# The end of a log-sum-exp kernel: clearing the semaphores on ScalarE during the last store, and waiting for that store behind the exit barriers

## The chip, the cores and the metric

The kernel runs on one core of a Trainium2 chip. The metric is the device time of one execution in microseconds; each time quoted is the median of several executions. The profile calls the engines PE (TensorE), DVE (VectorE), ACT (ScalarE), POOL (GpSimd) and SP (SyncE). All times inside a trace count from the start of the span, which is the time from the first to the last instruction of the program.

## The reference

```
def setup_inputs():
    batch, seq, dim = 32, 512, 1024
    return {"x": np.random.randn(batch, seq, dim).astype(np.float32), "axis": -1}

def reference(x, axis):
    x_max = np.max(x, axis=axis, keepdims=True)
    return (x_max.squeeze(axis) + np.log(np.sum(np.exp(x - x_max), axis=axis))).astype(np.float32)
```

There are 16,384 rows of 1,024 values: 67 MB come in and 64 KB go out.

## The kernel before

The rows are spread over 128 partitions, 128 rows on each. SyncE loads them in 17 chunks into a ring. ScalarE takes the exponentials; some rows are summed by ScalarE in the same instruction, the others by VectorE. Two logarithms, one early and one at the end, turn the sums into results, and ScalarE issues the one store:

```
    landed = [tc.alloc_semaphore(f"landed{i}") for i in range(len(CHUNKS))]
    act_done = tc.alloc_semaphore("act_done")
    dve_done = tc.alloc_semaphore("dve_done")
    stored = tc.alloc_semaphore("stored")
    # ... loads, exponentials, sums ...
    take_logs(logged, NB, dves, acts)
    nc.scalar.wait_ge(act_done, acts)
    nc.scalar.dma_start(out=out_v, in_=res).then_inc(stored, 16)
    nc.gpsimd.wait_ge(stored, 16)
    # ... the instruction lists are put in order; the function ends ...
```

What the program does behind its last line matters here. The semaphores came from the tile context, so the context's exit adds, after the wait: an all-engine barrier, a range clear on GpSimd that sets these 20 semaphores to zero (in the trace before, one update of each of the semaphores 99 to 118, from 161.765 to 161.856 us), and a second all-engine barrier. In such a barrier four engines each add one to a "gather" semaphore; GpSimd waits for all four, then adds four to a "release" semaphore, on which the others wait. For the first barrier the trace before shows four updates of semaphore 96 (the last, ScalarE's, at 160.212 us), GpSimd's decrement of it at 161.498 us, its addition to semaphore 97 at 161.576 us, and four decrements of that from 161.610 to 161.668 us.

The softmax here doesn't subtract the row's maximum and nothing guards it: scores larger than these inputs give would overflow.

## Time and profile before

| | before |
|---|---|
| time, median of 6 runs | 164.21 us (163.94 to 164.43) |
| span of the profiled run | 162.2 us |
| last logarithm ends | 159.61 us |
| store issued, and its last semaphore increment | 159.64, 161.215 us |
| last instruction ends | 162.18 us |

These are lines of the page of the kernel before: the span, the busy time of each engine with its share and number of instructions, and the chain of work that ended last.

```profile
span 162.2 us, 213 instructions
...
DVE 72.9 (45%) x11; ACT 124.1 (76%) x136; POOL 0.2 (0%) x4
...
ACT 52%; DMA 38%; DVE 7%; issue 1%
```

The loads bound the first part and ScalarE the second. The chain of waits of the kernel before shows this in order of time; its columns are start, duration (us), and what the chain ran through.

```profile
47.15 36.52 DMA ring<-in_x_dram
83.67 0.02 issue
83.69 10.55 ACT ring L128 x21
...
156.21 2.71 ACT ring L128 x5
158.91 0.22 issue
159.14 0.20 ACT ring L128
159.34 0.02 issue
159.36 0.25 ACT res L93
```

From about 84 us on, the chain stays on ScalarE, and it ends with the last logarithm (L93) at 159.61 us. But the span is 162.2 us. The last 2.6 us hold no counted work, so the chain and the shares of busy time don't describe them. The last two lines of the timeline of the kernel before (start, duration, engine, line, operation) show what is left:

```profile
159.36 0.25 ACT L93 ACTIVATE res<-sums 128x61 f32<-128x61 f32 x1
159.64 0.37 ACTq L140 DMA_DIRECT2D out_dram<-res  x1
```

The rest is barrier work, all of it put down to the line that launches the program (L189). These are six of the twelve lines of that line's view for the kernel before (left out are drains and semaphore instructions of other engines). In a barrier, the DRAIN of four engines carries their addition to the gather semaphore, and GpSimd has one ahead of its wait. The columns are engine, instruction, count, shortest/median/longest duration in ns, first and last start.

```profile
L189 POOLq EVENT_SEMAPHORE  x4: 17/17/17, 161.5 to 162.1; - x4
L189 POOLq DRAIN  x3: 34/41/83, 161.4 to 161.9; - x3
L189 ACTq DRAIN  x2: 8/80/152, 160.1 to 161.7; - x2
L189 PEldq EVENT_SEMAPHORE  x2: 51/51/51, 161.6 to 162.1; - x2
L189 POOLq COMPARE_BRANCH  x1: 33/33/33, 161.2 to 161.2; - x1
L189 POOLq EVENT_SEMAPHORE_RANGE_CLEAR  x1: 139/139/139, 161.7 to 161.7; - x1
```

GpSimd's branch at 161.2 carries the wait for the store. ScalarE was at the first barrier at 160.1 already (its first DRAIN), but everything of GpSimd's comes after 161.2. Taken one by one from the trace's instruction and semaphore records:

```
159.64  ScalarE  store issued (0.37 us)
160.21  ScalarE  gather mark of the first barrier
161.04 - 161.215 the store's 16 semaphore increments
161.24  GpSimd   wait for the store passes (branch), then a drain
161.58           first barrier released
161.74  GpSimd   range clear (0.14 us), then a drain
162.10           second barrier released
162.18  TensorE  last instruction ends: end of the span
```

From here on, the landing of the store is its last semaphore increment, at 161.215 here. So 0.96 us of serial work stand behind the landing, up to the end of the span. After the span the records show more: nine increments of semaphore 2 from 162.41 to 162.94, updates of many other semaphores from 162.83 on, then nine more increments of semaphore 2 from 163.73 to 164.083. No instruction of the program touches semaphore 2, so this text puts these increments down to the runtime; that is an inference. They are called its marks, the time from one to the next is a hop, the first nine are called the first closing barrier, and the stretch from the landing to the last mark is the tail. The reported time of this run is 163.96 us, 0.12 us less than the last mark.

### The profile page before, as it was taken

The page shows a single profiled execution, that of the slowest core. Times are in us where ns is not written, and L with a number is a line of the kernel's source. Part 1 is how long each engine was busy: PE and PEld are TensorE (multiplying, and loading weights), DVE is VectorE, ACT ScalarE, POOL GpSimd, SP SyncE. Part 2 cuts the span into 40 slices and gives each one's busy share as a digit, 9 for nine tenths or more (in the row PEclk, how much of TensorE's full clock was granted, in tenths as well). Part 3 has the DMA queues.
Part 4 walks back from the last instruction along what each step waited for, and adds up shares of the span by engine and source line. Part 5 has one row for each costly group of instructions (what it writes and reads, how often), then busy time and mean ns, then how long its engine had stood idle before and what let it go on. Part 6 is the DMA issues. An engine that isn't in the chain of part 4 may idle for free.

```text
span 162.2 us, 213 instructions
## 1 busy us (share of the span) xinstructions
DVE 72.9 (45%) x11; ACT 124.1 (76%) x136; POOL 0.2 (0%) x4
## 2 busy tenths in 40 slices
DVE  0030000039960799000999900000006999799591
ACT  3180006997099971999339999999999999999993
POOL 0000000000000000000000000000000000000000
DMA  6999899969969959969988999999999999999970
GB/s 263 497 485 470 349 394 517 485 291 517 485 291 517 517 259 517 517 275 501 517 368 370 424 424 432 461 497 388 436 427 399 431 400 439 420 424 414 415 318 16
DMA packets 2593, 67.18 MB, mean 414 GB/s; under 512 B 288, under 2 KB 416, under 8 KB 800
## 3 DMA queue, kind: packets, MB, share of 16 engines
q1 hardware_dynamic: 2448, 67.11, 96.4%
q10 hardware_dynamic: 144, 0.07, 0.1%
q14 instruction: 1, 0.01, 0.0%
HBM read 67.11 MB, written 0.07 MB: 414 GB/s over the span
## 4 chain that ended last, share of the span: by engine, by line
ACT 52%; DMA 38%; DVE 7%; issue 1%
DMA ring<-in_x_dram 38%; ACT ring L128 30%; ACT ring L116 22%; DVE sums L121 7%; ACT res L93 0%
## 5 line engine op out<-in xcount | busy, mean ns | idle before, releaser
L121 DVE TENSOR_REDUCE sums<-ring 128x5 f32<-128x5120 f32 (+8 forms) x11 | 72.9, 6648 | 86.0 <-ACT ring L116 85.9
L116 ACT ACTIVATE ring<-ring 128x5120 f32<-128x5120 f32 (+8 forms) x11 | 59.3, 5394 | 29.4 <-DMA ring<-in_x_dram 29.4
L128 ACT ACTIVATE ring<-ring 128x1024 f32<-128x1024 f32 x61 | 63.4, 1041 | 5.3 <-DMA ring<-in_x_dram 5.3
L128 ACT ACTIVATION_READ_ACCUMULATOR ring<-ring 128x1 f32 x61 | 11.4, 187 | 0.0
L103 ACT ACT_TABLE_LOAD x1 | 1.3, 1283 | 0.8 <-PEq L175 0.8
L93 ACT ACTIVATE res<-sums 128x67 f32<-128x67 f32 (+1 forms) x2 | 0.5, 256 | 0.1
L175 POOL MEMSET const-bfloat16-1.0<- 128x1 bf16 x1 | 0.1, 101 | 0.0
L175 POOL MEMSET const-uint8-127<- 128x1 uint8 x1 | 0.1, 101 | 0.0
L175 POOL MEMSET const-float32-0.0<- 128x1 f32 x1 | 0.1, 98 | 0.2 <-issue 0.2
L175 POOL MEMSET const-float32-1.0<- 128x1 f32 x1 | 0.1, 98 | 0.0
## 6 DMA issues: line engine op xcount, KB each, us to landing
ring<-in_x_dram SPq DMA_DIRECT2D x1, 7680.0 KB, 24.8
ring<-in_x_dram SPq DMA_DIRECT2D x1, 7168.0 KB, 36.1
ring<-in_x_dram SPq DMA_DIRECT2D x1, 6144.0 KB, 21.6
ring<-in_x_dram SPq DMA_DIRECT2D x1, 4608.0 KB, 32.1
ring<-in_x_dram SPq DMA_DIRECT2D x2, 2048.0 KB, 26.3
ring<-in_x_dram SPq DMA_DIRECT2D x1, 3584.0 KB, 40.2
ring<-in_x_dram SPq DMA_DIRECT2D x1, 2560.0 KB, 44.4
ring<-in_x_dram SPq DMA_DIRECT2D x2, 1024.0 KB, 46.0
```

Of the source, the lines that this page charges most:

```text
L93: nc.scalar.activation(out=res[:, lo:hi], in_=sums[:, lo:hi], func=Ln).then_inc(act_done, 1)
L103: nc.scalar.preload_act_table_set("natural_log_exp_and_others")
L116: nc.scalar.activation(out=ring[:, s : s + n_dve], in_=ring[:, s : s + n_dve], func=Exp).then_inc(act_done, 1)
L121: nc.vector.reduce_sum(out=sums[:, row : row + n_dve], in_=ring[:, s : s + n_dve], axis=AX).then_inc(dve_done, 1)
L128: nc.scalar.activation(out=ring[:, s + j], in_=ring[:, s + j], func=Exp, accum_out=sums[:, row + j : row + j + 1],).then_inc(act_done, 1)
L175: nc = _bacc.Bacc("TRN2", target_bir_lowering=False, num_devices=1)
```

## The change

The intent is to hide the clear and both barriers under the latency of the store. The semaphores are taken from the program, not from the tile context, so that the context's exit adds no clear. ScalarE clears them itself, right behind the issue of the store. The context is closed by hand, which puts its two barriers there, and only then does GpSimd wait for the store and count its semaphore back to zero.

```diff
-    landed = [tc.alloc_semaphore(f"landed{i}") for i in range(len(CHUNKS))]
-    act_done = tc.alloc_semaphore("act_done")
-    dve_done = tc.alloc_semaphore("dve_done")
-    stored = tc.alloc_semaphore("stored")
+    landed = [nc.alloc_semaphore(f"landed{i}") for i in range(len(CHUNKS))]
+    act_done = nc.alloc_semaphore("act_done")
+    dve_done = nc.alloc_semaphore("dve_done")
+    stored = nc.alloc_semaphore("stored")
+    used = sorted(sem.num for sem in [*landed, act_done, dve_done])
+    assert used == list(range(used[0], used[0] + len(used)))
 ...
     nc.scalar.dma_start(out=out_v, in_=res).then_inc(stored, 16)
-    nc.gpsimd.wait_ge(stored, 16)
+    nc.scalar.sem_clear(range(used[0], used[-1] + 1))
 ...
     nc.push_inst_callback(hook)
+    tc.close()
+    tc.compile()
+    nc.gpsimd.wait_ge(stored, 16)
+    nc.gpsimd.sem_inc(stored, -16)
```

The diff also folds a loop over one element (the parts of the first load) into a plain call, which changes no instruction. `stored` can't be in ScalarE's clear, as its increments are still to come: in the trace after, the clear's 19 updates come from 160.201 to 160.274 us, and the store's increments from 161.171 to 161.351 us.

More of the change, by code (lines that the diff above doesn't have):

```diff
@@ L16 @@
 LN_AT = 5
-FIRST_PARTS = [("sync", 0, 128)]
 @with_exitstack
@@ L83, in load @@
             nc.sync.wait_ge(act_done, act_wait)
-        for engine, lo, hi in FIRST_PARTS if i == 0 else [("sync", 0, P)]:
-            getattr(nc, engine).dma_start(
-                out=ring[lo:hi, s : s + r], in_=x_v[lo:hi, row : row + r]
-            ).then_inc(landed[i], 16)
+        nc.sync.dma_start(out=ring[:, s : s + r], in_=x_v[:, row : row + r]).then_inc(
+            landed[i], 16
+        )
     def take_logs(lo, hi, dve_wait, act_wait):
@@ L113 @@
             take_logs(0, logged, *done_before[i])
-        nc.scalar.wait_ge(landed[i], 16 * (len(FIRST_PARTS) if i == 0 else 1))
+        nc.scalar.wait_ge(landed[i], 16)
         if n_dve:
```

## The prediction

> **What bounds the kernel now.** The page gives a span of 162.2 us; the measured time is 164.2 us. Up to 94 us it follows its loads (page: DMA mean 414 GB/s, chain 38% DMA), and from there ScalarE: the chain of waits shows ScalarE Exp work almost without a gap from 95 us to 159.3 us. Up to the store the order of instructions is the same in both programs on every engine; only the tail differs.
>
> **The tail, from the trace's instruction and semaphore records (us from the span's start).** The last logarithm ends at 159.61 (timeline). ScalarE issues the store from 159.64 to 160.01; its sixteen increments arrive from 161.04 to 161.215, so 1.57 us pass from issue to completion. [...] Meanwhile GpSimd waits (released at 161.24), and all that follows is serial behind it: its branch and drain, the first exit barrier (release at 161.55), a drain, its range clear of the semaphores (161.74 to 161.88, 139 ns), the second barrier (release at 162.07), and the last engine's end at 162.18. That is 0.96 us from the store's last increment to the end of the span. After it the records show increments of semaphore 2 until 164.08[...].
>
> **What the change moves.** The range clear goes to ScalarE, directly behind the store's issue: about 0.14 us, while the store is under way. Both barriers then run during the store. Estimate from the durations above: ScalarE reaches the first barrier at about 160.35 instead of 160.21; from GpSimd's first gather to the second release took 0.60 us, of which the clear was about 0.2, so both barriers are through at about 160.8 to 161.0, still 0.2 to 0.4 us before the store's last increment at 161.215. What is left behind the store is one wait-and-decrement on GpSimd (17 ns), at about 161.24.
>
> **How much is on the critical path.** All of it: GpSimd's last instruction moves from 162.07–162.09 to about 161.24–161.26, by 0.83 us, and the span's end moves from 162.18 to about 161.26, by 0.9. The runtime's closing barrier takes the engines one after the other; in the trace before, its third increment comes 0.2 us after the second where all other like hops take about 0.04. If that late engine is GpSimd, the time gains 0.83; if it was another one that ends with the second barrier, up to 1.0.
>
> **Prediction.** 164.2 − 0.85 = 163.35 us. Range 163.1 to 163.8. Faster by over 2%: 0.01; within 2%: 0.98; slower by over 2%: 0.01.
>
> **What would show it.** Span of about 161.3. The timeline up to the store unchanged within 0.2 us. A range clear on ScalarE of about 0.14 us between the store's issue and its landing; both barriers' releases before the landing; GpSimd's last wait ending 20 to 50 ns after it. Time minus span stays at 1.8 to 2.0 us.
>
> **What would make it wrong.** (1) ScalarE's drain or clear waits for the store's descriptors, so that the barriers end after the landing[...]. (2) Engine-side work after each engine's last instruction is longest on GpSimd, so that time minus span grows: the gain would be less than 0.8. (3) The store's completion comes later because barrier traffic or the clear delays its increments. (4) The instruction stream shifts an instruction fetch into the busy part[...].

The sum, 164.2 − 0.85 = 163.35 us: its 0.85 us rest on times of the trace before, 0.83 us for GpSimd's last instruction and 0.9 us for the end of the span.

## The result, and the profile after

The changed kernel takes 163.37 us (median of 6 runs, 163.25 to 163.52) against 164.21 us (6 runs). The ratio is 0.995, with a 95% interval of 0.9938 to 0.9963.

The same lines of the page after: one instruction less (GpSimd's branch with the wait, three drains and the clear became two drains, one of them already at 0.74 us, and a wait; ScalarE got the clear), the same busy times, and 0.8 us less of span.

```profile
span 161.4 us, 212 instructions
...
DVE 72.9 (45%) x11; ACT 124.1 (77%) x136; POOL 0.2 (0%) x4
...
ACT 52%; DMA 38%; DVE 7%; issue 1%
```

The chain of waits after, the same stretch:

```profile
47.21 36.61 DMA ring<-in_x_dram
83.81 0.02 issue
83.84 10.56 ACT ring L127 x21
...
156.35 2.71 ACT ring L127 x5
159.06 0.22 issue
159.28 0.19 ACT ring L127
159.47 0.02 issue
159.50 0.25 ACT res L92
```

Nothing in the body moved, but the whole of it stands 0.14 us later in this execution: the first load landed at 7.52 us instead of 7.40 us, and the rest followed. This looks like scatter from run to run: in the twelve traces that end with this store, its issue lies anywhere from 159.55 to 160.06 us. Here it goes against the change. It is why the tails below are measured from the store's landing, not from the span's start. The last two lines of the timeline after:

```profile
159.50 0.25 ACT L92 ACTIVATE res<-sums 128x61 f32<-128x61 f32 x1
159.78 0.37 ACTq L139 DMA_DIRECT2D out_dram<-res  x1
```

The views of three lines after: the clear on ScalarE (L142), the two barriers (three of the ten lines of L162, where the context is closed), and GpSimd's wait for the store (L164).

```profile
L142 ACTq EVENT_SEMAPHORE_RANGE_CLEAR  x1: 119/119/119, 160.2 to 160.2; - x1
...
L162 POOLq EVENT_SEMAPHORE  x4: 17/17/17, 160.4 to 160.8; - x4
L162 ACTq DRAIN  x2: 8/8/8, 160.3 to 160.6; - x2
L162 PEldq EVENT_SEMAPHORE  x2: 51/51/51, 160.5 to 160.8; - x2
...
L164 POOLq EVENT_SEMAPHORE  x1: 17/17/17, 161.4 to 161.4; - x1
```

Before, GpSimd's barrier instructions ran from 161.5 to 162.1, behind the landing at 161.215. After, they run from 160.4 to 160.8, ahead of the landing, which is at 161.351 here. What is left behind it is one 17 ns wait on GpSimd.

The tail, from landing to the runtime's last mark, was 2.868 us before and is 2.035 us after: 0.83 us less, and the times of the runs say 0.84 us.

### The profile page after: what moved, and what is told of

Read it like the earlier page. It is cut to its first block, busy times and chain, and to the rows that moved or that the text cites. A ratio compares the mean times of both kernels' runs of the same rounds, so it can differ in the third digit from the quotient of the medians.

```text
span 161.4 us, 212 instructions
## 1 busy us (share of the span) xinstructions
DVE 72.9 (45%) x11; ACT 124.1 (77%) x136; POOL 0.2 (0%) x4
## 3 DMA queue, kind: packets, MB, share of 16 engines
q1 hardware_dynamic: 2448, 67.11, 97.0%
## 4 chain that ended last, share of the span: by engine, by line
ACT 52%; DMA 38%; DVE 7%; issue 1%
DMA ring<-in_x_dram 38%; ACT ring L127 30%; ACT ring L115 22%; DVE sums L120 7%; ACT res L92 0%
## 6 DMA issues: line engine op xcount, KB each, us to landing
ring<-in_x_dram SPq DMA_DIRECT2D x1, 2560.0 KB, 44.4
```

## The experiments

The theory (A): before, the barriers, the clear and GpSimd's way into the runtime's closing stood in series behind the landing; the change hides all but the last under the store's latency, and what does this is the place of the wait. The first rival (B): the gain is the clear, which leaves the chain between the barriers. The second question, raised by the traces, is what the 0.58 us are that lie between GpSimd's last instruction and the third mark of the runtime: 162.074 to 162.653 before, 161.376 to 161.954 after.

Each kernel was timed in five rounds beside the kernel before on the same chip, and gave a correct result unless said otherwise.

| run | time, us | ratio to before (95%) | landing to last mark, us |
|---|---|---|---|
| before | 163.99 to 164.26 | 1 | 2.868 |
| the change | 163.37 | 0.995 (0.9938 to 0.9963) | 2.035 |
| clear_only | 163.89 | 0.9976 (0.9959 to 0.9992) | 2.607 |
| wait_only | 163.33 | 0.9948 (0.9928 to 0.9967) | 2.033 |
| four_barriers | 164.23 | 0.9999 (0.9982 to 1.0015) | 2.881 |
| wait_on_sync | 162.90 | 0.9923 (0.9904 to 0.9943) | 1.477 |
| wait_on_tensor | 163.22 | 0.9940 (0.9927 to 0.9952) | 1.862 |
| wait_on_scalar | 163.15 | 0.9938 (0.9925 to 0.9952) | 1.647 |
| wait_on_vector | 162.88 | 0.9936 (0.9918 to 0.9954) | 1.620 |
| clear_between_sync | 162.95 | 0.9920 (0.9907 to 0.9934) | 1.633 |
| early_store_b (wrong) | 162.50 | 0.9896 (0.9883 to 0.9910) | no store at the end |
| after_again | 163.26 | 0.9952 (0.9939 to 0.9965) | 2.035 |
| wait_on_sync_again | 162.89 | 0.9925 (0.9911 to 0.9938) | 1.478 |

### One part alone: the clear, or the wait

clear_only keeps ScalarE's clear and puts the wait back ahead of the barriers:

```diff
     nc.scalar.sem_clear(range(used[0], used[-1] + 1))
+    nc.gpsimd.wait_ge(stored, 16)
+    nc.gpsimd.sem_inc(stored, -16)
 ...
-    tc.close()
-    tc.compile()
-    nc.gpsimd.wait_ge(stored, 16)
-    nc.gpsimd.sem_inc(stored, -16)
```

> The clear moves to ScalarE, but GpSimd still waits for the store ahead of the exit barriers. Theory A (the gain is the hidden serial tail): both barriers still stand behind the landing, only the clear between them is gone, whose removal shortened release-to-release from 0.52 to 0.33 us; so 0.2 us faster than before, 164.0 us, and the end of the span 0.75 us after the store's last increment. Rival B (the gain is the clear itself and its 19 semaphores, not the place of the wait): 163.4 us, as the full change.

It took 163.89 us, and its last mark came 2.607 us after the landing, 0.26 us earlier than before. GpSimd's wait (L144) and barrier instructions (L193) in this run still stand behind the landing, which was at 161.256 us:

```profile
L144 POOLq EVENT_SEMAPHORE  x1: 17/17/17, 161.3 to 161.3; - x1
...
L193 POOLq EVENT_SEMAPHORE  x4: 17/17/17, 161.4 to 161.9; - x4
```

Of the 0.26 us, 0.20 are the clear: from the first release to the second it took 0.33 us, against 0.52 us before. The other 0.07 us lie ahead of the first release (0.29 us after the landing instead of 0.36), where GpSimd has an event wait in place of the branch. So the change alters a third thing, the form of the wait: with the decrement behind it, it is no longer a branch. No run tests this apart from the place of the wait, so a share of about 0.07 us of the full gain may belong to it. The span's end was 0.70 us after the landing (expected: 0.75). Rival B, which needed 163.4 us, is ruled out by the tails (2.607 us against 2.035); the intervals of the ratios of clear_only and of the full change still overlap a little.

wait_only does the other part. All semaphores but `stored` come from the tile context again, so its exit clears them on GpSimd between the barriers, as before:

```diff
-    landed = [nc.alloc_semaphore(f"landed{i}") for i in range(len(CHUNKS))]
-    act_done = nc.alloc_semaphore("act_done")
-    dve_done = nc.alloc_semaphore("dve_done")
+    landed = [tc.alloc_semaphore(f"landed{i}") for i in range(len(CHUNKS))]
+    act_done = tc.alloc_semaphore("act_done")
+    dve_done = tc.alloc_semaphore("dve_done")
 ...
-    nc.scalar.sem_clear(range(used[0], used[-1] + 1))
```

> The wait goes behind the exit barriers, but the clear stays on GpSimd between them. Theory A: barriers plus clear still end at about 161.0, some 0.3 us before the landing, so the time is that of the full change, 163.4 us within 0.15. Rival B: the clear stays, so little is gained, about 164.0 us.

It took 163.33 us, and its last mark came 2.033 us after the landing: the full change to 2 ns. The second release fell 0.35 us before the landing, with the clear (0.54 us without it), so the clear on GpSimd costs nothing there. GpSimd's lines in this run show the clear and the barriers (L161) ahead of the landing at 161.349 us, and the wait (L163) behind it:

```profile
L161 POOLq EVENT_SEMAPHORE  x4: 17/17/17, 160.4 to 161.0; - x4
...
L161 POOLq EVENT_SEMAPHORE_RANGE_CLEAR  x1: 138/138/138, 160.6 to 160.6; - x1
...
L163 POOLq EVENT_SEMAPHORE  x1: 17/17/17, 161.4 to 161.4; - x1
```

The title of the change names two parts; with the wait on GpSimd, the second alone, with the decrement that it needs, makes the gain.

### How much room is under the store

four_barriers adds four barriers to the full change, ahead of the last wait:

```diff
     tc.close()
     tc.compile()
+    for _ in range(4):
+        nc.all_engine_barrier()
     nc.gpsimd.wait_ge(stored, 16)
```

> The full change with four more all-engine barriers ahead of the last wait. A barrier takes 0.33 us from release to release, and 0.57 us lie between the second release and GpSimd's wake by the store. Theory A: 4 x 0.33 - 0.57 = 0.74 us slower than the full change, about 164.1 us, and GpSimd's last wait ends at once after the last release. A rival by which each barrier always costs its time: 1.3 us slower, 164.7 us; one by which barriers during the store are free: 163.4 us.

It took 164.23 us, 0.86 us more than the full change (2.881 − 2.035 = 0.85 us by the marks). The view of the added line in this run, and GpSimd's instructions alone:

```profile
L164 POOLq EVENT_SEMAPHORE  x8: 17/17/17, 160.9 to 162.0; - x8
L164 POOLq DRAIN  x4: 34/34/34, 160.8 to 161.8; - x4
```

The landing was at 161.26 us, so the barriers ran past it and decided the end. The sum was right in kind and 0.11 us short: the four barriers took 1.35 us from release to release (three of 0.33 us and one of 0.37 us, which met the landing; why that one was longer isn't settled), and the room is about 0.50 us, not 0.57 us, since GpSimd's wait came 0.07 us after its own release. Both rivals missed: the barriers are neither free nor charged whole. By this one run they are free up to a room of 0.50 us, with the wait on GpSimd.

### What is left: the store's latency

early_store_b asks what the store still costs. It is wrong: SyncE stores the first half of the results into both halves of the output, before the last load, and ScalarE's store at the end is gone.

```diff
+        if i == len(CHUNKS) - 1:
+            half = NB // 2
+            nc.sync.wait_ge(act_done, logs_done)
+            for k in range(2):
+                nc.sync.dma_start(
+                    out=out_v[:, k * half : (k + 1) * half], in_=res[:, :half]
+                ).then_inc(stored, 16)
 ...
     nc.scalar.wait_ge(act_done, acts)
-    nc.scalar.dma_start(out=out_v, in_=res).then_inc(stored, 16)
 ...
-    nc.gpsimd.wait_ge(stored, 16)
-    nc.gpsimd.sem_inc(stored, -16)
+    nc.gpsimd.wait_ge(stored, 32)
+    nc.gpsimd.sem_inc(stored, -32)
```

> Wrong result on purpose: SyncE stores the first half of the results into both halves of the output before the last load, some 50 us before the end, so no wait for a store is left at the end; the rest is the full change. Theory: then the clear, two barriers and GpSimd's 0.58 us alone make the tail; from the end of ScalarE's last logarithm to the last mark of the runtime 2.65 us instead of 3.64 us, so the store's latency is still worth about 0.95 us after the change: 162.4 us[...]. Rival (something other than the store holds the end now): 163.4 us, tail unchanged.

It took 162.50 us. From the end of the last logarithm to the last mark it was 2.735 us, against 3.635 us in the full change: 0.90 us are still the store's. The views of its clear (L149) and of GpSimd's wait (L171), which now follows the second release (160.44 us) without waiting:

```profile
L149 ACTq EVENT_SEMAPHORE_RANGE_CLEAR  x1: 114/114/114, 159.8 to 159.8; - x1
...
L171 POOLq EVENT_SEMAPHORE  x1: 17/17/17, 160.5 to 160.5; - x1
```

The expectation had the stores done some 50 us before the end. In fact they landed at 157.28 us. They went through the queue of the loads (q1: 2,736 packets; before it was 2,448, with the store in q10), and issue to landing took 44.4 us; the loads in the lines next to theirs in the DMA view took 46.4 and 44.0 us. The landing is still 3.2 us before the wait, so the reading holds.

A first draft of this kernel had SyncE's stores behind the last load: SyncE's wait on `act_done` was then not ordered ahead of ScalarE's clear of it, a race on `act_done`. A condition for the change itself: the engine that clears must come after every other engine's wait on those semaphores. What happens otherwise, no run shows. In the changed kernel this holds because SyncE's last wait stands before the last load (issued at 112.46 us in the trace after) and ScalarE waits for that load (158.34 us), and because ScalarE waits for VectorE's last sum (159.04 us), all ahead of the clear at 160.18 us.

### Which engine should wait last

wait_on_sync is the full change with another engine in the last two lines:

```diff
-    nc.gpsimd.wait_ge(stored, 16)
-    nc.gpsimd.sem_inc(stored, -16)
+    nc.sync.wait_ge(stored, 16)
+    nc.sync.sem_inc(stored, -16)
```

> The full change, with the last wait on SyncE instead of GpSimd. Theory A1: GpSimd needs 0.58 us from its last instruction to its mark in the runtime's closing barrier (both traces), other engines about 0.25 us, so the wait sits on the slowest engine; on SyncE the time falls by 0.2 us (if SyncE stands early in the closing chain) to 0.45 us (if last): 162.9 to 163.2 us. Rival A2: the 0.58 us is a delay of the runtime that follows the last engine whichever it is: no change, 163.4 us.

The 0.25 us for the other engines was an estimate: of these, the two traces at hand show TensorE's alone, 0.23 us from its end to the first mark. This run took 162.90 us, faster than the full change by 0.47 us (a paired run follows below), and by 0.56 us in the tail. It was run at another time. Rival A2 (0.58 us whichever engine comes last) is ruled out: SyncE's mark came 0.15 us after the start of its wait. Its view:

```profile
L164 SPq EVENT_SEMAPHORE  x1: 17/17/17, 161.3 to 161.3; - x1
```

wait_on_tensor, wait_on_scalar and wait_on_vector put `tensor`, `scalar` and `vector` in the same two lines.

> The full change, with the last wait on TensorE. Reading of the closing barrier so far: its marks go through the five engines one after the other[...], so what runs ahead of the late engine is done early and what follows it is still to come. If TensorE is first in that chain (its mark came 0.23 us after its end in the trace of the full change), its mark comes 0.31 us after the landing and all eight hops follow: closing barrier done 0.68 us after the landing, against 0.89 (GpSimd) and 0.33 (SyncE) measured: about 163.15 us. Rival (every engine but GpSimd is alike): as on SyncE, 162.9 us.

> The full change, with the last wait on ScalarE. If ScalarE is second in the closing chain: mark at about 0.27 us after the landing, closing barrier done about 0.61 us after it, time about 163.1 us, between TensorE and SyncE. Rival (every engine but GpSimd is alike): 162.9 us.

> The full change with the last wait on VectorE, which should be fourth of five in the closing chain (TensorE first, ScalarE second, GpSimd third, SyncE last, as the late mark showed). Its mark comes 0.15 to 0.33 us after its wait, as on ScalarE and TensorE, and about 0.24 us of hops follow: closing barrier done 0.41 to 0.59 us after the landing, between SyncE (0.33) and GpSimd (0.89): about 163.0 us.

They took 163.22, 163.15 and 162.88 us. The time of wait_on_vector scatters (162.63 to 163.51 us), so it can't be ranked by its time; the marks can rank it. Here are the nine marks of the first closing barrier in each run, in us from the landing, and the start of the last wait:

```
wait on   wait    1       2       3       4       5       6      7      8      9
TensorE   0.029   0.359*  0.393   0.431   0.475   0.499   0.596  0.635  0.669  0.716
ScalarE   0.021  -0.226   0.178*  0.216   0.260   0.283   0.382  0.420  0.454  0.501
GpSimd    0.025  -0.230  -0.195   0.603*  0.646   0.670   0.769  0.807  0.843  0.890
VectorE   0.028  -0.240  -0.205   0.000   0.232*  0.255   0.354  0.392  0.426  0.473
SyncE     0.016  -0.231  -0.197   0.008   0.051   0.167*  0.211  0.250  0.284  0.330
```

The starred mark is the one that the late engine holds back: it comes later after the mark ahead of it than in the other rows (TensorE's, which has none ahead of it, comes later after the landing). It moves one place to the right from row to row. So the first five marks go through TensorE, ScalarE, GpSimd, VectorE and SyncE. Which engines the other four belong to, no run shows. Two things set the cost of an engine that comes last: how long it needs from its wait to its mark (TensorE 0.33, ScalarE 0.16, GpSimd 0.58, VectorE 0.20, SyncE 0.15 us), and how many marks still follow (0.36 us of hops after TensorE's mark, 0.32 after ScalarE's, 0.29 after GpSimd's, 0.24 after VectorE's, 0.16 after SyncE's). SyncE is best in both, though only just in the first. GpSimd's 0.58 us (0.578 to 0.580) are the same in the eleven traces in which no earlier engine holds its mark up, whether its last instruction is a barrier's or the wait; what it does in that time isn't shown. The rival by which all engines but GpSimd are alike is ruled out by the marks. The times alone rank little: the intervals of the ratios of TensorE, ScalarE and VectorE overlap, also with that of the full change.

With the wait on SyncE, GpSimd's own mark falls together with the landing (0.008 us), so the way through the barriers is by now nearly as long as the store. clear_between_sync is wait_only with the wait on SyncE; it asks whether the clear's place matters there. It was run at another time.

> The clear stays on GpSimd between the exit barriers and the last wait is on SyncE. With the wait on SyncE, GpSimd's mark came only 0.01 us after the landing, so its chain is as long as the store's latency; the clear put back there lengthens it by 0.20 us. Theory: closing barrier done 0.06 to 0.12 us later than with the clear on ScalarE (0.39 to 0.45 us after the landing instead of 0.33), the time about 163.0 us: here the clear's place costs something, while with the wait on GpSimd it cost nothing. Rival (the clear is always hidden): 0.33 us.

The closing barrier was done 0.487 us after the landing, not 0.330, so ScalarE's clear is worth 0.16 us here, more than the expected 0.06 to 0.12 us: GpSimd's mark came 0.20 us later, as expected, but the hops from there on took 0.28 us, where I had counted less. The marks show where: the hop from the fifth mark to the sixth took 0.044 us with SyncE late, but 0.098 us here. Why it differs isn't shown. The times (162.95 and 162.90 us) don't resolve this; it rests on one trace each, and the spread of the same tail between repeated runs was 1 ns or less.

Last, the full change and the version with SyncE once more, as they had run on different chips.

> The full change once more, on the same chip as the next run, so that the two can be told apart: 0.84 us faster than before, ratio 0.995.

> The wait on SyncE once more, beside the full change: 0.5 us faster than it (0.56 us by the trace's last marks), so 1.3 to 1.4 us faster than before, ratio 0.992; a rival by which the difference was one of chips: the same as the full change.

The ratios to before were 0.9952 and 0.9925, which is 0.45 us between the two kernels by their means, and the tails of the traces came out as before (2.035 and 1.478 us). So the version with the wait on SyncE beats both kernels. The medians alone, 163.26 and 162.89 us, are 0.37 us apart. The difference of the times is somewhat below that of the tails (0.56 us); the intervals of the ratios, which just don't touch, allow for it.

## Why the prediction was right

- The predicted time was 163.35 us, and 163.37 us were measured. The gain of 0.85 us was measured as 0.84 us.
- That "both barriers are through at about 160.8 to 161.0": the second release came at 160.81 us. wait_only and four_barriers show that barriers and clear are hidden, and how much more would be.
- "ScalarE reaches the first barrier at about 160.35 instead of 160.21": it did at 160.352 us, but the agreement is luck. The whole body stood 0.14 us later; from the landing its mark came 1.00 us ahead in both kernels. Before, ScalarE's drain behind the issue of the store took 152 ns; after, the clear (119 ns) stands in that time and the drain takes 8 ns. So the clear on ScalarE cost no time of its own, where the estimate had 0.14 us for it.
- "If that late engine is GpSimd, the time gains 0.83": it is GpSimd, by the table of marks, and the tail got 0.83 us shorter.
- The span was predicted at about 161.3 us and is 161.4 us; the body that stood 0.14 us later accounts for this. Time minus span is 1.88 us (range given: 1.8 to 2.0).
- Of the four things that could have made it wrong, none hurt. Neither clear nor drain held ScalarE up (its mark in the first barrier came 1.00 us ahead of the landing); the store took 1.57 us in both kernels, so the barriers didn't delay it; the way into the closing code is indeed longest on GpSimd, but its 0.58 us were in the time before too and cancelled (time minus span did grow, from 1.78 to 1.88 us, because TensorE's end, at 162.18 us before and 160.89 us after, no longer closes the span; the estimate of 0.83 us had allowed for that); of a moved instruction fetch the traces show nothing (one in the span, at 89 us, in both).
- "All other like hops take about 0.04": in the trace before they took 0.023 to 0.046 us, save the one from the fifth mark to the sixth, with 0.099 us. The third mark, 0.205 us after the second, still stands out.
- On what the store's 1.57 us consist of: by the packet records of the kernel before, the first data packet starts 0.87 us after the issue, the packets take 0.35 us, and the last increment comes 0.35 us after the last packet's end. Most of it lies ahead of the data. No number of the prediction hung on that.
- The text credits both parts of the change alike. The experiments split them: clear_only shortens the tail by 0.26 us (0.20 by the clear, 0.07 by the form of the wait), the wait alone by 0.83 us, both together by 0.83 us.

## What to carry to other kernels

Work that only tidies up (clears, exit barriers) ran under the latency of the last store here (1.57 us) once the wait for that store was the last thing in the program; that is worth 0.83 us, and with the wait on GpSimd there is room for about 0.5 us more before the tidying shows again. Ask also which engine waits last: what follows was not the same for all of them here (0.15 us from the wait to the mark on SyncE, 0.58 us on GpSimd), and moving two lines from GpSimd to SyncE gave another 0.45 us by the mean times and 0.56 us by the tails. There the room is nearly used up: putting the clear back between the barriers lengthened the tail by 0.16 us. For effects of about 0.5% measure a tail from an event inside the trace, such as the landing of the store, once the stretch ahead of it is seen to be unchanged (issue to landing took 1.57 us before and after). In two repeated pairs it came out within 1 ns, where whole runs scattered by 0.3 us and more.
